# FFN stages of a two-layer encoder: residual sums, load times, the place of the statistics and the order of the last pair

## The chip, the cores and the metric

The kernel runs on one core of a Trainium2 chip in a single launch. The metric is the device time of that launch in microseconds (us). Three runs of the kernel before gave 2211.5, 2214.02 and 2214.56 us, so the median is 2214.02.

## The reference

Two encoder layers run on 512 tokens of width 1024 in float32. Each layer is an FFN at half weight, a mixer (attention of two kinds), cross-attention to a memory of 256 tokens, and a second half-weight FFN, all with an RMS norm ahead and a residual behind:

```python
def rmsnorm(x, g):
    y = xf * lax.rsqrt(jnp.mean(xf * xf, axis=-1, keepdims=True) + EPS)
    return (y * g)
def swiglu(x, wg, wu, wd):
    return (jax.nn.silu(x @ wg) * (x @ wu)) @ wd

for layer in range(2):
    h = h + 0.5 * swiglu(rmsnorm(h, g), wg, wu, wd)          # FFN 1, inner width 2816
    h = h + mixer(rmsnorm(h, mix_g), ...)
    h = h + memory_xattn(rmsnorm(h, mg), rmsnorm(mem, sg), ...)
    h = h + 0.5 * swiglu(rmsnorm(h, g2), wg2, wu2, wd2)      # FFN 2
```

## The kernel before

Activations lie transposed, as eight tiles `x[k]` of 128 features by 512 tokens. Each float32 operand is split into a rounded part and a remainder (`xh` and `xl`, `wh` and `wl`), and a product is three matmuls: high by high, high by low, low by high. ACT makes the high part (for weights L153 or L398, for activations L201), DVE the low part (L155, L399, L203), and in some places POOL takes a share of L155. The two lists `LEAD` and `REST` of the change name these products: (0, 0) and (0, 1) use the weight's high part, (1, 0) its low part.

There are four FFN stages: from 0 to 389 us, from 783 to 1148, from 1148 to 1500 and from 1842 to the end. The mixer and the cross-attention stand between them. A stage has three kinds of work on the tensor engine (PE):

- `plain_pair` computes the first 256 inner features by ordinary matmuls (L309, 128x512): block `b=0` has 48, and `b=1` has 24 for the gate weights `wg` and 24 for `wu`. Between the two halves of `b=1` it calls `stats`: four matmuls by `ident` sum the residual's squares `acc` over the features (`column_sums`, L247), DVE reduces them (L249) and scales them (L256, `v`), and POOL raises `v` to the power -1/2 (L240, `r`). After `b=1`, four more transposes (L318) spread `r` to the tile `R` (L320), by which gate values are multiplied.
- Pairs 1 to 10 use seven products of half-size blocks in place of eight. `open_pair`, `sum_pair`, `cross_pair` and `close_pair` issue one to three products of 24 matmuls (128x256, L417). Their activations are sums and differences of halves of the tokens, made by `token_sums` (L357 `tq`, L361, L364, L366: `t1h`, `t1l` to `t4l`). Their weights are quarters `wq`, loaded by `raw_quarter` (L407) or, for `s1` and `s3`, loaded by SP (L446, L471) and added to by an accumulating DMA of POOL (L447, L473). For `s3`, ACT flips the sign between the two (L472).
- `down` multiplies the finished hidden values `hh` and `hl` by the down weights in three chunks of 8, 8 and 6 inner blocks (L535), eight output blocks `d` in each; L542 and L543 add the result to the residual, and in the last chunk `made` starts the next stage's `xh` and the squares.

The squares are taken by ACT (L216, L219) and added by DVE or POOL (L220) into `acc`. In `out_proj`, at the end of the mixer and of the cross-attention, `sums` does all eight at the end on DVE.

PE follows the program. For DVE, ACT, POOL and SP a scheduler chooses the order, by the order of the program, by priorities (`high_priority`) and by `behind(x)`, which lets an instruction come only after `x`. On each engine the instructions then start in that order. Buffers come round: `wf` has three, `wh` and `wl` two, and `sh` and `sl`, used by every third operand of a pair, one.

Of the kernel before, what the change touches and what calls it, by code (L numbers as in the profile page):

```python
# [19 lines left out]
P = 128  # L20
# [43 lines left out]
PAD_SMALL = 80  # L64

# [37 lines left out]
class Encoder:  # L103
# [45 lines left out]
    def wfill(self, tiles, src, sl, eng, after=None):  # L149
        nc = self.nc  # L150
        w, wh, wl = tiles
        dma = nc.sync.dma_start(w[:, sl], src[:, sl])
# [26 lines left out]
    def load_x(self, srcs):  # L179
# [15 lines left out]
        self.sums()  # L195
# [10 lines left out]
    def sums(self):  # L206

        for x in self.x:
            with self.behind(self.lead), self.behind(self.rest):
                self.acc = self.square(self.acc, x, S, eng=self.nc.vector)  # L210

    def square(self, acc, x, n, pool=None, eng=None):
        nc = self.nc
        if acc is None:
            acc = (pool or self.xp).tile([P, S], F32, name="acc", tag="acc", bufs=1)
            nc.scalar.activation(acc[:, :n], x, AF.Square)  # L216
        else:
            sq = self.xp.tile([P, S], F32, name="sq", tag="sq", bufs=2)
            nc.scalar.activation(sq[:, :n], x, AF.Square)  # L219
            (eng or nc.gpsimd).tensor_add(acc[:, :n], acc[:, :n], sq[:, :n])  # L220
# [18 lines left out]
    def rsqrt(self, out, v, n):  # L239
        self.nc.gpsimd.tensor_tensor(out, v, self.mhalf[:, :n], op=OP.pow)  # L240
# [20 lines left out]
    def ffn(self, pre):  # L261


        with ExitStack() as ctx:
            pool = lambda name: ctx.enter_context(self.tc.tile_pool(name=pre + name, bufs=1))
            f = self.f = SimpleNamespace(pre=pre, hp=pool("h"), tp=pool("t"), H={}, n=0, last=None)
            self.plain_pair()
            if self.mem_r is None:
                self.mem_stats()
            ends = [sum(CHUNKS[:c + 1]) // 2 for c in range(len(CHUNKS))]  # L270
            c = 0
            pair = self.open_pair(1)
            for p in range(1, FB // 2):
                final = p == FB // 2 - 1
                self.sum_pair(pair)
                if p - 1 in [e - 1 for e in ends]:
                    self.down(c)
                    c += 1
                self.cross_pair(pair, final)
                old, pair = pair, None if final else self.open_pair(p + 1)  # L280
                self.close_pair(old, final)
            self.down(c)

    def plain_pair(self):
# [4 lines left out]
        for b in range(2):  # L289
# [3 lines left out]
            pp = [self.bank("pa"), self.bank("pa")] if b == 0 else [self.bank2(), self.bank2()]  # L293
# [11 lines left out]
            for ks, ops in groups:  # L305
                for w, p in zip(ws, pp):
# [133 lines left out]
    def sum_pair(self, pair):  # L440
# [3 lines left out]
        with self.tc.high_priority():  # L444
            pair.s = f.tp.tile([P, 1024], F32, name="s1", tag="s1", bufs=2)
            nc.sync.dma_start(pair.s, self.quarter(p, 3))  # L446
# [9 lines left out]
    def cross_pair(self, pair, final):  # L456
        nc, f, p = self.nc, self.f, pair.p

        def own():
            with self.tc.high_priority():  # L460
                pair.w12 = self.raw_quarter(p, 1)
                w = self.operand(pair.w12)
            x = self.bank("pa")
            self.product(x, w, f.B["21"], True)
            c = self.corner(pair, 0, 0)
            nc.vector.tensor_add(c, c, self.halves(x))

        def other():
            with self.tc.high_priority():
                s = f.tp.tile([P, 1024], F32, name="s3", tag="s3", bufs=2)  # L470
                nc.sync.dma_start(s, self.quarter(p, 2))  # L471
                nc.scalar.activation(s, s, AF.Copy, scale=-1.0)  # L472
                nc.gpsimd.dma_start(s, self.quarter(p, 0), accum_op=OP.add)  # L473
                w = self.operand(s)
            self.product(pair.y, w, f.B["3"], False)
            c = self.corner(pair, 1, 1)
            nc.scalar.copy(c, self.halves(pair.y))
# [1014 lines left out]
```

## Time and profile before

| | |
|---|---|
| median of the runs | 2214.02 us (2211.5 to 2214.56) |
| the profiled execution | 2214.37 us, span 2212.6 us |
| busy: PE, DVE, ACT, POOL | 95%, 71%, 52%, 15% |
| granted clock of the span, mean | 0.984 |

PE is busy in nearly all of the span. The other 5% is idle time of PE, and the profile's list of waits says who ended it. A granted clock of 0.5 is the lower of two levels (1.2 against 2.4 GHz). PE busy time counts modelled ends, so a matmul of 128x512 in a row of its own shows 0.39 us, though the next starts 0.227 us later (24 of them take 5.44 us).

### The profile page before, as it was taken

Reading aid. Unit: us, or ns where it says so; the run is one execution under the profiler, and the core shown is the slowest. Engines: PE = TensorE matmul, PEld = TensorE weight load, DVE = VectorE, ACT = ScalarE, POOL = GpSimd, SP = SyncE. Lnnn points to the kernel's source line nnn. Section 1 sums busy time; section 2 is a strip of 40 time slices with the busy share of each in tenths; the row PEclk is TensorE's granted clock in tenths of the full one; section 3 lists DMA queues with packets and bytes.
Section 4 is the critical chain, followed back from the end, with each engine's and each line's share of the span. In section 5 each row is a group of like instructions: output and inputs, shape, how many; then the busy total and the mean of one; then the engine's idle time right before and its main releaser. Section 6 shows DMA issues by size and latency. Waiting matters only on the chain.

```text
span 2212.6 us, 32535 instructions
## 1 busy us (share of the span) xinstructions
PE 2111.8 (95%) x12830; PEld 1881.5 (85%) x12834; DVE 1573.5 (71%) x2255; ACT 1139.7 (52%) x1701; POOL 339.6 (15%) x306
## 2 busy tenths in 40 slices
PE   4999999999999879999999999999999987999998
PEld 3989998887778769898989899988888876989897
DVE  5767767479876678586788677674668676857666
ACT  4535434465685556253455345344678554635442
POOL 1100001336441100000020000003453011000000
PEclk8999999999999999999999999999999998999999
DMA  6546633421232247375346456334223214546632
GB/s 203 147 128 164 172 105 115 143 81 62 77 122 73 73 124 189 102 186 150 93 137 183 133 162 171 106 110 155 79 86 128 93 58 133 164 123 174 160 103 88
DMA packets 86121, 279.65 MB, mean 126 GB/s; under 512 B 9680, under 2 KB 12880, under 8 KB 85968
## 3 DMA queue, kind: packets, MB, share of 16 engines
q1 hardware_dynamic: 74448, 235.62, 32.1%
q0 software_dynamic: 11520, 41.95, 10.7%
q8 instruction: 101, 1.65, 0.3%
q14 instruction: 52, 0.43, 0.1%
HBM read 271.24 MB, written 6.29 MB: 125 GB/s over the span
## 4 chain that ended last, share of the span: by engine, by line
PE 88%; DVE 7%; DMA 2%; ACT 1%; issue 1%; SPq 0%; DVEq 0%; ACTq 0%
PE ps_pa L417 26%; PE ps_pb L535 11%; PE ps_pa L535 10%; PE ps_pb L417 10%; PE ps_pa L628 10%; PE ps_pa L580 4%; PE ps_pa L309 2%; PE ps_pb L734 2%; PE ps_pa L1166 2%; PE ps_pa L1025 2%; PE ps_pb L786 1%; PE ps_pb L759 1%; PE ps_pa L944 1%; PE ps_pb L309 1%; PE ps_pb L580 1%
## 5 line engine op out<-in xcount | busy, mean ns | idle before, releaser
L153 ACT ACTIVATE wh<-wf 128x1024 fp32r<-128x1024 f32 (+2 forms) x215 | 219.1, 1019 | 380.5 <-PE ps_pb L535 112.7
L155 DVE TENSOR_TENSOR wl<-wf,wh 128x1024 fp32r<-128x1024 f32 (+2 forms) x174 | 202.9, 1168 | 63.6 <-ACT wh L153 62.9
L399 DVE TENSOR_TENSOR wl<-s,wh 128x1024 fp32r<-128x1024 f32 x104 | 127.2, 1223 | 86.5 <-ACT wh L398 64.1
L398 ACT ACTIVATE wh<-s 128x1024 fp32r<-128x1024 f32 x104 | 110.0, 1058 | 114.5 <-PE ps_pb L417 29.4
L398 ACT ACTIVATE wh<-wf 128x1024 fp32r<-128x1024 f32 x84 | 89.1, 1061 | 109.6 <-PE ps_pb L535 23.5
L535 PE MATMUL ps_pb<-hh,wl 128*128 128x512 f32 x352 | 137.8, 392 | 5.4 <-DVE wl L155 5.4
L535 PE MATMUL ps_pa<-hh,wl 128*128 128x512 f32 x352 | 137.8, 392 | 5.4 <-DVE wl L155 5.4
L535 PE MATMUL ps_pb<-hh,wh 128*128 128x512 f32 x352 | 137.6, 391 | 0.0
L535 PE MATMUL ps_pa<-hh,wh 128*128 128x512 f32 x352 | 137.5, 391 | 0.0
L535 PE MATMUL ps_pa<-hl,wh 128*128 128x512 f32 x352 | 137.3, 390 | 0.0
L535 PE MATMUL ps_pb<-hl,wh 128*128 128x512 f32 x352 | 137.3, 390 | 0.0
L155 POOL TENSOR_TENSOR wl<-wf,wh 128x1024 fp32r<-128x1024 f32 x41 | 99.7, 2431 | 176.4 <-ACT wh L153 148.9
L628 PE MATMUL ps_pa<-wh,xh 128*128 128x512 f32 x384 | 123.3, 402 | 0.0
L473 POOL DMA_DIRECT2D s<-l_ffn_wq x40 | 35.6, 890 | 569.2 <-ACT s L472 569.2
L628 PE MATMUL ps_pa<-wh,xl 128*128 128x512 f32 x384 | 119.9, 394 | 0.0
L628 PE MATMUL ps_pa<-wl,xh 128*128 128x512 f32 x384 | 119.5, 393 | 0.0
L542 DVE TENSOR_TENSOR dn<-ps_pb,R 128x512 f32<-128x512 f32 x48 | 33.1, 690 | 100.3 <-PE ps_pb L535 100.3
L542 DVE TENSOR_TENSOR dn<-ps_pa,R 128x512 f32<-128x512 f32 x48 | 33.1, 690 | 100.3 <-PE ps_pa L535 100.3
L447 POOL DMA_DIRECT2D s<-l_ffn_wq x40 | 34.7, 868 | 443.8 <-DMA s<-l_ffn_wq 303.8
L399 DVE TENSOR_TENSOR wl<-wf,wh 128x1024 fp32r<-128x1024 f32 x84 | 102.6, 1222 | 0.0
L399 DVE TENSOR_TENSOR sl<-s,sh 128x1024 fp32r<-128x1024 f32 x56 | 68.5, 1223 | 33.1 <-ACT sh L398 33.0
L628 PEld LDWEIGHTS ps_pa<-wh,xl 128*128 128x128 f32 x384 | 72.7, 189 | 16.0
(372 smaller groups left out, 5946.0 us busy)
## 6 DMA issues: line engine op xcount, KB each, us to landing
wf<-l_ffn_wq SPq DMA_DIRECT2D x120, 512.0 KB, 3.4
s<-l_ffn_wq SPq DMA_DIRECT2D x80, 512.0 KB, 4.2
s<-l_ffn_wq POOLq DMA_DIRECT2D x80, 512.0 KB, 6.8
wf<-l_ffn_wd SPq DMA_DIRECT2D x64, 512.0 KB, 3.8
wf<-l_w_in SPq DMA_DIRECT2D x48, 512.0 KB, 3.2
wf<-l_ffn_wd SPq DMA_DIRECT2D x32, 384.0 KB, 3.1
wf<-l_mem_wkv SPq DMA_DIRECT2D x16, 512.0 KB, 3.2
wf<-l_w_out SPq DMA_DIRECT2D x16, 512.0 KB, 3.3
```

What stands on the lines that cost most here:

```text
L153: nc.scalar.activation(wh[:, sl], w[:, sl], AF.Copy)
L155: eng.tensor_sub(wl[:, sl], w[:, sl], wh.bitcast(F32)[:, sl])
L309: nc.tensor.matmul(p, w[a][:, k * P:(k + 1) * P], xs[k][c], start=k == order[0] and a == c == 0, stop=k == order[-1] and a == 1)
L398: nc.scalar.activation(h, t, AF.Copy)
L399: nc.vector.tensor_sub(l, t, h.bitcast(F32))
L417: self.nc.tensor.matmul(bank[:, sl], w[a][:, o:o + P], xs[k][b], start=first and z == a == b == k == 0, stop=z == a == 1 and k == KB // 2 - 1,
L535: nc.tensor.matmul(bank, w[a][:, j * P:(j + 1) * P], hs[e], start=j == a == e == 0, stop=j == nb - 1 and e == 1)
L542: nc.vector.tensor_mul(t, bank, f.R)
L580: nc.tensor.matmul(banks[dd], a[:, o:o + P], parts(k)[b], start=k == first and a is wh and b == 0, stop=k == last and a is wl)
L628: nc.tensor.matmul(banks[i], xs[k][a][:, i * P:(i + 1) * P], w[b][:, kk * 512:kk * 512 + 512], start=k == a == b == 0, stop=k == KB - 1 an ...
L734: nc.tensor.matmul(bank[:, o:o + n], a, b[:, :n], start=c == 0, stop=c == len(ops) - 1)
L1025: nc.tensor.matmul(banks[c][i], a[:, i * P:(i + 1) * P], b[:, c * 512:(c + 1) * 512], start=(k == 0 and n == 0), stop=(k == KB - 1 and n = ...
```

## The change

- `sums` is called in `out_proj` for four residual tiles at a time, behind their `made`: first for group 1, with the additions on POOL, then for group 0 on DVE. The squares have high priority.
- `token_sums` is called after both blocks of the plain pair, behind the last square and the last addition.
- `stats` comes after the plain pair and no longer between the halves of `b=1`. The part that makes `R` (`plain_end`) is called after `open_pair(1)`.
- The quarter loads (`fetch`) come behind the last load of the plain pair. The memory's statistics (`mem_stats`) come after pair 2.
- The last pair computes "21" (`own`) before "3" as the other pairs do. The first down block of the last chunk goes to `sh` and `sl`, and its eight `LEAD` matmuls come ahead of `close_pair`; the last pair's own operands there all use `wh` and `wl`.
- Inside a chunk the products are grouped: `LEAD` of all inner blocks, then `REST`, then the same for the chunk's last two inner blocks.

```diff
-    def sums(self):
-        for x in self.x:
-            with self.behind(self.lead), self.behind(self.rest):
-                self.acc = self.square(self.acc, x, S, eng=self.nc.vector)
+    def sums(self, xs, eng):
+        with self.behind(self.lead), self.behind(self.rest), self.tc.high_priority():
+            for x in xs:
+                self.acc = self.square(self.acc, x, S, eng=eng)
@@ ffn
-            self.plain_pair()
-            if self.mem_r is None:
-                self.mem_stats()
+            R = self.plain_pair()
...
             pair = self.open_pair(1)
+            R()
...
-                self.cross_pair(pair, final)
-                old, pair = pair, None if final else self.open_pair(p + 1)
-                self.close_pair(old, final)
-            self.down(c)
+                self.cross_pair(pair)
+                if final:
+                    early = self.block(c, 0, True)
+                    self.down_products(c, early, LEAD, False)
+                    self.close_pair(pair, True)
+                    self.down(c, early)
+                else:
+                    old, pair = pair, self.open_pair(p + 1)
+                    self.close_pair(old, False)
+                if p == 2 and self.mem_r is None:
+                    self.mem_stats()
@@ plain_pair
-                    if b == 1 and p is pp[0]:
-                        v, r = self.stats(self.acc, QB)
-            if b == 0:
-                with self.behind(self.lead), self.behind(self.rest):
-                    self.token_sums()
-        p = self.bank2()
+        f.after = self.loaded
+        with self.behind(self.summed), self.behind(self.squared):
+            self.token_sums()
+        v, r = self.stats(self.acc, QB)
+        return lambda: self.plain_end(banks, r)
@@ quarter loads
+    def fetch(self, t, p, q):
+        with self.behind(self.f.after):
+            self.nc.sync.dma_start(t, self.quarter(p, q))
+        return t
@@ down
-        early = [block(d) for d in range(2)]
-        for w, bank in early:
-            products(bank, w, range(nb - 2))
-        for d, (w, bank) in enumerate(early):
-            products(bank, w, range(nb - 2, nb))
-            done(d, bank)
+        early = [first or self.block(c, 0), self.block(c, 1)]
+        for b in early[first is not None:]:
+            self.down_products(c, b, LEAD, False)
+        for b in early:
+            self.down_products(c, b, REST, False)
+        for d, b in enumerate(early):
+            self.down_products(c, b, LEAD + REST, True)
+            done(d, b[1])
@@ out_proj
+            if done:
+                self.sums(self.x[4 * g:4 * g + 4], nc.gpsimd if g else nc.vector)
...
-        self.sums()
```

SP issues the loads of the first stage in this order before (`wf` from `l_ffn_wq` and every `s_` tile are quarters of the pairs):

```order
L193 DMA x<-xT 128x512
L471 DMA s_545<-l_ffn_wq 128x1024
L193 DMA x<-xT 128x512
L471 DMA s_777<-l_ffn_wq 128x1024
L152 DMA wf<-l_ffn_wg 128x512
L193 DMA x<-xT 128x512
L125 DMA cols<-cols 128x92
L193 DMA x<-xT 128x512
L446 DMA s_452<-l_ffn_wq 128x1024
L152 DMA wf<-l_ffn_wu 128x512
L446 DMA s_684<-l_ffn_wq 128x1024
L152 DMA wf<-l_ffn_wg 128x1024
```

The same place, the first loads of SP, now:

```order
L195 DMA x<-xT 128x512
L127 DMA cols<-cols 128x92
L195 DMA x<-xT 128x512
L154 DMA wf<-l_ffn_wg 128x512
L195 DMA x<-xT 128x512 x2
L154 DMA wf<-l_ffn_wu 128x512
L195 DMA x<-xT 128x512
L154 DMA wf<-l_ffn_wg 128x1024
L195 DMA x<-xT 128x512 x2
L154 DMA wf<-l_ffn_wg 128x512
L154 DMA wf<-l_ffn_wu 128x512
L195 DMA x<-xT 128x512
```

The four `s_` loads have left the head of SP's queue; they now stand behind the last load of `wu`, which is two rows further on.

In the second FFN stage (l0_ffn2), DVE had this order between the token sums and `R` before:

```order
L364 TENSOR_TENSOR t3l<-tq,t3h 128x1024
L357 SCALAR_TENSOR_TENSOR tq<-x,cols,tq 128x256 x3
L399 TENSOR_TENSOR wl<-wf,wh 128x1024
L220 TENSOR_TENSOR acc<-acc,sq 128x512
L364 TENSOR_TENSOR t2l<-tq,t2h 128x1024
L364 TENSOR_TENSOR t4l<-tq,t4h 128x1024
L220 TENSOR_TENSOR acc<-acc,sq 128x512 x3
L249 TENSOR_REDUCE s<-ps_pb 128x4
L256 TENSOR_SCALAR v<-s 128x4
L399 TENSOR_TENSOR wl<-s_7711,wh 128x1024
L320 COPY R<-ps_pb 128x512
```

DVE at the same place now, where the additions into `acc` have all gone before:

```order
L375 TENSOR_TENSOR t3l<-tq,t3h 128x1024
L411 TENSOR_TENSOR wl<-wf,wh 128x1024
L375 TENSOR_TENSOR t2l<-tq,t2h 128x1024
L411 TENSOR_TENSOR wl<-s_7711,wh 128x1024
L251 TENSOR_REDUCE s<-ps_pb 128x4
L375 TENSOR_TENSOR t4l<-tq,t4h 128x1024
L466 TENSOR_TENSOR s_7711<-s_7711,wf 128x1024
L411 TENSOR_TENSOR wl<-wf,wh 128x1024
L258 TENSOR_SCALAR v<-s 128x4
L411 TENSOR_TENSOR sl<-s_7711,sh 128x1024
L503 TENSOR_TENSOR s_7711<-wf,s_7711 128x1024
L331 COPY R<-ps_pb 128x512
```

The additions have gone from the place ahead of the reduce, and weight remainders, one of them of the accumulated tile `s_7711`, have come ahead of the reduce and of `v`.

At the end of the first stage (l0_ffn1), ACT had this order in the last pair before (128x768 are down weights, `gu` are products copied out of PSUM, the second L344 and L507 belong to the pair's second half):

```order
L153 ACTIVATE wh<-wf 128x768
L507 ACTIVATE t<-gs 128x512
L153 ACTIVATE wh<-wf 128x768
L490 COPY gu<-ps_pa 128x2x256
L344 ACTIVATE hh<-gs 128x512
L507 ACTIVATE t<-gs 128x512
L344 ACTIVATE hh<-gs 128x512
L153 ACTIVATE wh<-wf 128x768 x2
```

ACT at the same place now:

```order
L488 COPY gu<-ps_pa 128x2x256
L155 ACTIVATE wh<-wf 128x768 x2
L516 ACTIVATE t<-gs 128x512
L499 COPY gu<-ps_pa 128x2x256
L355 ACTIVATE hh<-gs 128x512
L516 ACTIVATE t<-gs 128x512
L355 ACTIVATE hh<-gs 128x512
L155 ACTIVATE wh<-wf 128x768
```

The weights of a second and a third down block are both converted ahead of the first `t` of the last pair, where one stood ahead of it before.

## Rows read from the trace of the kernel before

**Rows 1.** The page: busy time, share of the span, instructions of each engine.

```profile
PE 2111.8 (95%) x12830; PEld 1881.5 (85%) x12834; DVE 1573.5 (71%) x2255; ACT 1139.7 (52%) x1701; POOL 339.6 (15%) x306
```

**Rows 2.** Waits of PE, whole span: us in total, times, longest.

```profile
PE ps_pb L247 <- DVE acc L220: 38.8, 5, 10.3
...
PE ps_pa L535 <- DVE wl L155: 5.4, 6, 1.0
PE ps_pb L535 <- DVE wl L155: 5.4, 6, 1.0
PE ps_pa L417 <- ACT gu L454: 4.8, 4, 1.2
```

**Rows 3.** Stretch 0 to 31: us, engines' busy time, clock, DMA share, GB/s.

```profile
0.00:31.00 31.00, 11.61 (x28) 7.86 (x29) 8.68 (x21) 11.65 (x17) 4.30 (x10) 0.87 0.93 277
```

**Rows 4.** Timeline of SP, first stage: start, us, operation.

```profile
17.41 0.33 SPq L193 DMA_DIRECT2D x<-xT  x1
...
30.03 0.33 SPq L152 DMA_DIRECT2D wf<-l_ffn_wu  x1
```

**Rows 5.** Timeline of PE, first stage; in brackets idle time and its releaser.

```profile
51.34 1.09 PE L247 MATMUL ps_pb<-ident,acc 128*128 128x128 f32 x4 [9.19 <-DVE acc L220]
...
65.06 0.64 PE L417 MATMUL ps_pb<-t1h,wh 128*128 128x256 f32 x4
```

**Rows 6.** Timeline of DVE, third stage (l1_ffn1).

```profile
1152.60 6.03 DVE L357 SCALAR_TENSOR_TENSOR tq<-x,cols,tq 128x256 f32<-128x256 f32 x15
...
1163.48 1.22 DVE L364 TENSOR_TENSOR t2l<-tq,t2h 128x1024 fp32r<-128x1024 f32 x1
...
1166.88 0.68 DVE L249 TENSOR_REDUCE s<-ps_pb 128x4 f32<-128x512 f32 x1
```

**Rows 7.** Timeline of POOL, third stage.

```profile
1154.30 0.88 POOL L447 DMA_DIRECT2D s<-l_ffn_wq  x1 [5.15 <-DVE tq L357]
...
1167.86 1.03 POOL L240 TENSOR_TENSOR r<-v,mhalf 128x4 f32<-128x4 f32 x1 [5.90 <-DVE v L256]
```

**Rows 8.** Timeline of PE, second, third and fourth stage.

```profile
812.86 1.11 PE L247 MATMUL ps_pb<-ident,acc 128*128 128x128 f32 x4 [10.34 <-DVE acc L220]
...
824.57 0.64 PE L417 MATMUL ps_pb<-t1h,wh 128*128 128x256 f32 x4
...
1176.07 0.64 PE L417 MATMUL ps_pb<-t1h,wh 128*128 128x256 f32 x4
...
1883.74 0.64 PE L417 MATMUL ps_pb<-t1h,wh 128*128 128x256 f32 x4
```

**Rows 9.** Stretch with the lower clock behind the stall of the second stage.

```profile
807.80:818.00 10.20, 5.14 (x14) 4.22 (x15) 5.31 (x8) 1.26 (x2) 1.04 (x1) 0.50 0.01 2
```

**Rows 10.** Timeline of PE, cross-attention of both layers.

```profile
728.50 1.11 PE L247 MATMUL ps_pb<-ident,acc 128*128 128x128 f32 x4 [4.90 <-DVE acc L220]
...
1787.59 1.11 PE L247 MATMUL ps_pb<-ident,acc 128*128 128x128 f32 x4 [4.63 <-DVE acc L220]
```

**Rows 11.** Timeline of PE, chunks and last pair of the first stage.

```profile
143.65 0.50 PE L535 MATMUL ps_pb<-hh,wl 128*128 128x512 f32 x1 [0.94 <-DVE wl L155]
...
355.27 0.40 PE L535 MATMUL ps_pb<-hh,wh 128*128 128x512 f32 x1
...
364.79 0.50 PE L535 MATMUL ps_pb<-hh,wl 128*128 128x512 f32 x1 [0.74 <-DVE wl L155]
```

**Rows 12.** Timeline of ACT, last pair of the first stage.

```profile
354.04 0.63 ACT L507 ACTIVATE t<-gs 128x512 f32<-128x512 f32 x1 [4.16 <-DVE gs L505]
355.04 0.85 ACT L153 ACTIVATE wh<-wf 128x768 fp32r<-128x768 f32 x1 [0.37 <-PE ps_pa L417]
...
358.38 0.63 ACT L507 ACTIVATE t<-gs 128x512 f32<-128x512 f32 x1 [1.49 <-DVE gs L505]
...
360.50 0.63 ACT L344 ACTIVATE hh<-gs 128x512 fp32r<-128x512 f32 x1 [1.49 <-DVE gs L509]
```

**Rows 13.** Issues of DMAs, 1149 to 1163: size, median us to landing.

```profile
s<-l_ffn_wq POOLq DMA_DIRECT2D x4, 512.0 KB, 11.5
```

More of the change, by code (lines that the diff above doesn't have):

```diff
@@ L64 @@
 PAD_SMALL = 80
+LEAD, REST = ((0, 0), (0, 1)), ((1, 0),)
 CHUNKS = (8, 8, 6)
@@ L454, in sum_pair, with cross_pair @@
         nc.scalar.copy(self.corner(pair, 0, 1), self.halves(pair.y))
-    def cross_pair(self, pair, final):
+    def cross_pair(self, pair):
         nc, f, p = self.nc, self.f, pair.p
[L459 to L477, printed above, removed]
-            nc.vector.tensor_add(c, c, self.halves(pair.z))
-        for step in (other, own) if final else (own, other):
-            step()
+        with self.tc.high_priority():
+            pair.w12 = self.raw_quarter(p, 1)
+            w = self.operand(pair.w12)
+        x = self.bank("pa")
+        self.product(x, w, f.B["21"], True)
+        c = self.corner(pair, 0, 0)
+        nc.vector.tensor_add(c, c, self.halves(x))
+        with self.tc.high_priority():
+            s = f.tp.tile([P, 1024], F32, name="s3", tag="s3", bufs=2)
+            self.fetch(s, p, 2)
+            nc.scalar.activation(s, s, AF.Copy, scale=-1.0)
+            nc.gpsimd.dma_start(s, self.quarter(p, 0), accum_op=OP.add)
+            w = self.operand(s)
+        self.product(pair.y, w, f.B["3"], False)
+        c = self.corner(pair, 1, 1)
+        nc.scalar.copy(c, self.halves(pair.y))
+        nc.vector.tensor_add(c, c, self.halves(pair.z))
     def close_pair(self, pair, final):
         nc, f, p = self.nc, self.f, pair.p
+        own = False if final else None
         def lower():
             with self.tc.high_priority():
-                w = self.operand(self.raw_quarter(p, 3))
+                w = self.operand(self.raw_quarter(p, 3), own)
             self.product(pair.y, w, f.B["4"], False)
@@ L494, in upper @@
                 nc.vector.tensor_sub(pair.s, pair.w12, pair.s)
-                w = self.operand(pair.s)
+                w = self.operand(pair.s, own)
             self.product(pair.z, w, f.B["22"], False)
@@ L521, in close_pair, with block, down_products, down @@
         self.hidden_parts(p, gs, 0)
[L523 removed]
+    def block(self, c, d, own=False):
         nc, f = self.nc, self.f
[L527 to L538 removed]
+        n = CHUNKS[c] * P
+        src = self.I[f.pre + "wd"][d, :, sum(CHUNKS[:c]) * P:sum(CHUNKS[:c]) * P + n]
+        if not own:
+            return self.wload(src, n), self.bank2()
+        with self.tc.high_priority():
+            w = self.wp.tile([P, 1024], F32, name="wf", tag="wf", bufs=3)
+            h, l = [f.tp.tile([P, 1024], F32R, name=t, tag=t, bufs=1) for t in ("sh", "sl")]
+            self.wfill((w, h, l), src, slice(0, n), nc.vector)
+        return (h, l), self.bank2()
+    def down_products(self, c, block, ops, tail):
+        f = self.f
+        (w, bank), nb = block, CHUNKS[c]
+        for a, e in ops:
+            for j in range(nb - 2, nb) if tail else range(nb - 2):
+                b = sum(CHUNKS[:c]) + j
+                h = f.H[b // 2][e][:, b % 2 * S:b % 2 * S + S]
+                self.nc.tensor.matmul(bank, w[a][:, j * P:(j + 1) * P], h, start=j == a == e == 0,
+                                      stop=j == nb - 1 and (a, e) == ops[-1])
+    def down(self, c, first=None):
+        nc, f = self.nc, self.f
+        last = c == len(CHUNKS) - 1
         def done(d, bank):
```

57 lines of the change are left out of this document (26 added, 31 removed).

## The prediction

> **What bounds the kernel now.** I read the page first: PE is busy for 2111.8 of 2212.6 us [rows 1], so a change that adds no matmul is worth at most the idle time of PE and the time that its lower clock costs. The list of waits then says who ended that idle time [rows 2]. The largest item, 38.8 us in five waits, are the four transposes of L247, which wait for the last addition into `acc`. Next come 10.8 us in twelve waits for the low part `wl` of a down weight, and 4.8 us in four for a copy of the product "2" in the last pair. A matmul count is unchanged by the edit, so I take the stages one at a time, each by the moment when PE starts the product T1 (`ps_pb<-t1h`), the first that needs all of the stage's statistics to be out of its way.
>
> **Start of the first stage.** DMA is busy for 0.93 of the first 31 us at 277 GB/s [rows 3]; 4.2 MB of that are the four `s` loads and their four accumulating loads. The last `x` is issued at 17.41 and the last `wu` at 30.03 [rows 4]. Then the squares are added late among the token sums, PE stands 9.19 us, and T1 starts at 65.06 [rows 5]. Now `x`, `cols`, `wg` and the first `wu`, 3.6 MB in all, go first. At 277 GB/s and some 2 us for the first to land they need 3.6 / 0.277 + 2 = 15 us. The last `xh` and `xl` are then ready at about 17, block `b=0` ends near 22.5 and `b=1` (10.9 us) near 34, with its column sums behind it at 34.6 and `open_pair` (24 matmuls, 2.88 us) at 37.3. No stall for `acc` is left. What is late next is `R`: between the last addition (near 26) and `v`, DVE now has 16 `tq` at 0.40, nine instructions of 1024 columns at 1.14 from one start to the next, and the reduce at 0.68 [rows 6], that is 6.4 + 10.3 + 0.7 = 17.4, so 43.5 at the earliest. ACT must feed them in its own order, behind two `s3` loads and three memory tiles, for which I add 2 us. With 1.03 for the power on POOL [rows 7], T1 starts near 46.5, after a new PE stall of some 9 us. That is 18.5 us sooner. A stall of that length was followed by 0.50 of the clock for 10.2 us, half of it in the stall [rows 9], so 2.5 us are lost again: **-16 us**, and between -10 (ACT held by the loads) and -27 (`R` hidden behind `open_pair`, T1 at 38).
>
> **Start of both second FFN stages.** T1 starts at 824.57 and 1883.74, after stalls of 10.34 us [rows 8] and 9.7 (38.8 less the other four of its five waits) for `acc`. The additions now follow the last `xl` (near 790) on DVE, four at 0.69 with two weights of 1.2 between, and are done near 795.7, so `b=1` follows `b=0` without a gap: it ends near 805.6, `open_pair` near 809.5. DVE's queue again holds `v` back: from 795.7, 16 `tq` (6.4), nine of 1024 columns (10.3), and the reduce (0.7) make 813.1, one of the nine waits for ACT's conversion behind `open_pair` (+1), and the power takes 1.03, so T1 starts near 817. The stall changes its place and shrinks from 10.3 to some 7. 7.5 us sooner, less 2.5 of clock, is **-5** for the first; the second's stall was 0.6 shorter, and I take **-4**. Each lies between 0 and -14. The third stage, l1_ffn1, had no stall for `acc`. There the reduce comes to stand behind a weight that needs the end of `b=1`, so T1 stays at 1176.07 [rows 8] within a microsecond: 0.
>
> The accumulating DMA is the cover that can fail here. In the third stage, where the `s` loads already follow the last `wu`, POOL issues the first accumulation at 1154.30, 4 us after the `s` load, and it lands 11.5 us later by the median [rows 7, 13]. In l0_ffn2 the `s` loads would go out near 790.6, when `b=0` frees a buffer for the last `wu`, so `s1` is whole near 806, and DVE reaches its `wl` near 808: 2 us to spare.
>
> **Cross-attention.** PE waits 4.90 and 4.63 us for `acc` [rows 10], and for the half clock behind them I add 1.6 and 1.4, part of the 2.5 that followed the longer stall. With four additions on POOL ahead and four on DVE early, `acc` is whole when PE comes, by my count to within a microsecond. **-6.5 and -6**; if POOL is late with its weights, half of that.
>
> **Chunks.** In chunks 1 and 2 PE waits 0.94 [rows 11] and 1.0 at the second matmul of the third block, since `wl` is used there. With LEAD first, `wl` is used 12 matmuls (2.7 us) later, so the wait goes. Over four stages 4 x 1.94 = **-7.8**. Nothing else is late there, as `wh` was ready.
>
> **The last pair.** Two waits go: 1.2 for the copy, since "21" now stands between, and 0.76 at the last chunk [rows 11], as the second block no longer shares a buffer with the first. But the cover of the last gate half is shorter. Before, 24 matmuls (5.4 us) ran from 355.27 until `hh` was needed, and `hh` was done at 361.13 [rows 11, 12], just in time. Now eight have moved ahead, and 16 (3.63 us) are left. Furthermore ACT's order puts two weight conversions before the first `t`, and the second needs the buffer that the product "4" frees at its end, E. The row of before at 355.04 shows that such a conversion waits for PE at the head of ACT's queue [rows 12]. From E: the conversion 0.85, on DVE its `wl` 0.95, which stands ahead of `t` there, two steps of 0.69, `hh` 0.63, then `hl` and `gs` 1.4, `t` 0.63, two steps 1.4, and the second `hh` 0.63, with 0.3 for the semaphores: E + 8.1. PE needs it at E + 3.63 + 0.23. The stall is 4.2, and 0.2 more for `hl`: 4.4 in place of 1.96, that is +2.4 in each stage, **+9.8**. If the clock falls behind it, as it did after 4.63, up to 2 more each (+8). The other end is the chain of before, 5.9 us from E, a stall of 2.0: 0.
>
> The Trainium skill states in "Perfetto Trace Analysis" (Tensor Engine Instruction) that ACT, DVE and GpSimd are strict FIFO. It speaks against this change at this place: by it the `t` waits for the end of product "4" though its own input is there. If ACT could pass the waiting conversion, the last pairs would come to 0 and the whole to about 2169. The row at 355.04 agrees with the rule as far as it goes; what stands behind the conversion there needed the same event.
>
> **The memory's statistics** (eight squares, seven additions) leave the start for pair 2, with ACT 52% and POOL 15% busy [rows 1]: 0. POOL's and DVE's shares of `wl` in the mixers shift by one tile in places, 1.2 us either way at single blocks: 0, within 4.
>
> **Sum.** -16 - 5 - 4 - 12.5 - 7.8 + 9.8 = -35.5. The profiled execution took 2214.4, which is 0.4 over the median: **2179 us**.
>
> **Rivals.**
> - *R is no longer waited for.* If DVE and ACT run through the start without waits, T1 comes at the end of `open_pair`: -27, -14, -13 in the three stages, and no half clock. With the rest as above 2214.4 - 54 - 12.5 - 7.8 + 9.8 = 2150. For it: the third stage, with its statistics in the middle, starts T1 without a stall for `acc`, so DVE can keep up where nothing is added to its queue. Against it: seven instructions stand ahead of `v` that did not before. Half of it gives 2164.
> - *The stalls only change place.* The starts gain 10, 0 and 0, one cross-attention keeps half of its wait (3), and the half clock follows each last pair (+8): 2214.4 - 10 - 9.5 - 7.8 + 17.8 = 2205. For it: 2 us to spare at `s1`, and a stall of over 4 us in each last pair.
> - *Slower: the accumulated quarter holds DVE.* `wl<-s1` stands ahead of the reduce, in order. From the point where `s1` lands more than 2 us after my count, each microsecond moves `R`, and PE with it, in the three starts. To lose 35.5 us and more it has to be 12 + 2 us later in each, 29 us from the load's issue in place of 15; the time would be 2220. Against it: the 11.5 us of [rows 13] were under a full load of the third stage.
> - *It doesn't do what it says.* If loads still crowd the start and POOL's additions come as late as DVE's did, the last pairs' +9.8 cancels the chunks' -7.8 and the time stays at 2214.
>
> **Chances.** The forecast, 2168 to 2192, 0.52; R not waited for, 2150 to 2168, 0.19; stalls change place, 2192 to 2209, 0.22; slower 0.04; no effect 0.03. A measurement of this kernel tells 0.2% (4.4 us) from no change. So faster 0.93, same 0.03, slower 0.04. The range 2160 to 2202 leaves out the outer part of both neighbours.
>
> **What would show it.** In the profile after: T1 near 46.5, 817 less what was gained before, and the same for the fourth stage; PE idle before L329's transposes, released by POOL's `r`, and none before L249; no wait for `wl` in the chunks but one of some 4 us for `hh` at the end of each stage, with ACT's second `wh` starting when product "4" ends. The first step fails if the last `x` lands after 20 us or PE waits for DMA at T1; the forecast is wrong if the four last pairs stall under 2 or over 7 us, or if the new stall at `R` exceeds 12.

## The result and the profile after

The changed kernel takes 2184.72 us (median of 4 runs, 2184.33 to 2187.51) against 2213.43 for the kernel before on the same chip: 0.9874 of it, with an interval from 0.9857 to 0.9891, or 28.7 us less. The profiled execution took 2184.71 us with a span of 2182.9. The page of after gives PE less busy time than in [rows 1] and a larger share of the span:

```profile
PE 2105.0 (96%) x12834; PEld 1881.6 (86%) x12834; DVE 1571.6 (72%) x2242; ACT 1138.4 (52%) x1701; POOL 361.1 (17%) x319
```

The waits of PE (us in total, times, longest) show what took the place of [rows 2]:

```profile
PE ps_pb L329 <- POOL r L242: 25.6, 4, 12.5
PE ps_pa L553 <- ACT hh L355: 14.9, 4, 3.7
...
PE ps_pb L432 <- DVE gu L489: 3.0, 4, 0.7
PE ps_pb L249 <- DVE acc L222: 2.9, 2, 2.5
```

The 38.8 us for `acc` have become 2.9. The 10.8 us for `wl` and the 4.8 for the product "2" are gone. New are 25.6 us for `r`, 14.9 for the last pair's `hh`, and 3.0 for `gu` at the last pair's product "22".

To see where the time went I set the same products of both traces side by side (T1, T2 and so on of every pair) and read by how much the later trace leads. Each piece of the program then has one number:

| piece | forecast | measured |
|---|---|---|
| start of the first stage, up to T2 | -16 | -13.2 (T1 alone -15.5) |
| eight chunks with two blocks ahead (1 and 2 of each stage) | -7.8 | -10.8 |
| four last pairs with the third chunk | +9.8 | +16.9 (3.6, 5.0, 3.7, 4.6) |
| cross-attention, layers 0 and 1 | -6.5, -6 | -6.5, -4.0 |
| starts of l0_ffn2 and l1_ffn2 | -5, -4 | -6.5, -5.8 |
| l1_ffn1's start and both mixers | 0 | 0.0 |
| sum | -35.5 | -29.9 |

The spans differ by 29.7. The 0.0 is a sum of small pieces: the mixer of layer 0 lost 0.5, the memory's column sums in pair 2 another 0.2, and l1_ffn1's start and the mixer of layer 1 gained 0.3 each.

**First stage.** The timeline of PE (start, us, operation; in brackets the idle time ahead and its releaser) answers to [rows 5]:

```profile
32.82 0.60 PE L249 MATMUL ps_pb<-ident,acc 128*128 128x128 f32 x4
...
48.80 1.11 PE L329 MATMUL ps_pb<-ident,r 128*128 128x128 f32 x4 [12.52 <-POOL r L242]
49.57 1.20 PE L432 MATMUL ps_pb<-t1h,wh 128*128 128x256 f32 x4
```

The plain pair ends at 32.8, where the forecast had 34, and no time is lost at `acc`. All that is left stands at `r`. ACT and DVE show why it comes at 48.8 and not at 45:

```profile
29.54 0.42 ACT L218 ACTIVATE acc<-mem 128x256 f32<-128x256 f32 x1 [3.27 <-DMA mem<-memT]
...
35.73 1.04 ACT L372 ACTIVATE t1h<-tq 128x1024 fp32r<-128x1024 f32 x1
```

```profile
36.81 1.22 DVE L377 SCALAR_TENSOR_TENSOR t1l<-tq,t1h 128x1024 fp32r<-128x1024 f32 x1 [3.85 <-ACT t1h L372]
...
46.55 0.16 DVE L258 TENSOR_SCALAR v<-s 128x4 f32<-128x4 f32 x1
```

Three squares of the memory stand ahead of `t1h` on ACT, each waits for its load (3.27, 1.57 and 2.51 us, 7.35 together), and DVE in turn stands 3.85 us for `t1h`. Behind `t1l` ten more instructions of DVE come before `v`. The power on POOL behind `v` took 1.95 us, where [rows 7] have 1.03.

**Second FFN stage.** PE, and DVE between the reduce and `v` (with [rows 8]):

```profile
797.58 1.11 PE L329 MATMUL ps_pb<-ident,r 128*128 128x128 f32 x4 [6.06 <-POOL r L242]
```

```profile
791.31 0.70 DVE L251 TENSOR_REDUCE s<-ps_pb 128x4 f32<-128x512 f32 x1
791.91 1.23 DVE L375 TENSOR_TENSOR t4l<-tq,t4h 128x1024 fp32r<-128x1024 f32 x1
793.04 1.24 DVE L466 TENSOR_TENSOR s<-s,wf 128x1024 f32<-128x1024 f32 x1
794.18 1.24 DVE L411 TENSOR_TENSOR wl<-wf,wh 128x1024 fp32r<-128x1024 f32 x1
795.31 0.18 DVE L258 TENSOR_SCALAR v<-s 128x4 f32<-128x4 f32 x1
```

Three instructions of 1.13 us each, from one start to the next, hold `v` back for 3.4 of the 6.06 us. They were in the order printed ahead of the prediction. Another 0.9 is the power, which takes 1.95 us here too, beside an instruction of DVE that had begun 0.18 us before it:

```profile
795.40 1.23 DVE L411 TENSOR_TENSOR sl<-s,sh 128x1024 fp32r<-128x1024 f32 x1
795.58 1.95 POOL L242 TENSOR_TENSOR r<-v,mhalf 128x4 f32<-128x4 f32 x1 [10.86 <-DVE v L258]
```

The same holds at the starts of the first and the fourth stage (both 1.95). Before, the power took 1.04 at all three, and DVE stood idle. Why it takes longer is not shown.

The two starts of FFN 2 also gained at a place that the forecast did not look at. Before, PE waited 2.04 us for `xh` at the first products of l0_ffn2 (2.01 at l1_ffn2). On ACT two sign flips of `s3` stood among the eight `xh`:

```profile
782.86 1.06 ACT L472 ACTIVATE s<-s 128x1024 f32<-128x1024 f32 x1
```

```profile
785.53 0.50 PE L309 MATMUL ps_pa<-xh,wh 128*128 128x512 f32 x1 [2.04 <-ACT xh L201]
```

With the quarter loads behind the last `wu`, the flips come later, and the longest wait there is 0.44 (0.45 at l1_ffn2). At matched products this is 1.8 of the 6.5 us in l0_ffn2 and some 2 of the 5.8 in l1_ffn2.

**Cross-attention of layer 1.** The wait of [rows 10] has shrunk from 4.63 to 2.51 us there, and to 0.37 in layer 0:

```profile
1763.68 0.66 PE L249 MATMUL ps_pb<-ident,acc 128*128 128x128 f32 x4 [2.51 <-DVE acc L222]
```

DVE, ahead of it, has the last additions between the next step's low parts:

```profile
1760.61 0.68 DVE L222 TENSOR_TENSOR acc<-acc,sq 128x512 f32<-128x512 f32 x1
1761.21 0.68 DVE L1116 TENSOR_TENSOR xql<-ps_pa,xqh 128x512 fp32r<-128x512 f32 x1
1761.82 1.21 DVE L157 TENSOR_TENSOR wl<-wf,wh 128x1024 fp32r<-128x1024 f32 x1
1762.95 0.68 DVE L222 TENSOR_TENSOR acc<-acc,sq 128x512 f32<-128x512 f32 x1
```

**Chunks.** In the first chunk, where [rows 11] had 0.94 us for `wl`, the third block now runs through:

```profile
142.85 1.52 PE L553 MATMUL ps_pa<-hh,wl 128*128 128x512 f32 x6
```

**Last pair of the first stage**, PE, ACT and DVE (for ACT before, [rows 12]):

```profile
334.88 0.74 PE L432 MATMUL ps_pb<-xh,wh 128*128 128x256 f32 x4 [0.74 <-DVE gu L489]
...
344.39 0.45 PE L553 MATMUL ps_pa<-hh,sh 128*128 128x512 f32 x1
348.57 0.80 PE L553 MATMUL ps_pa<-hh,sh 128*128 128x512 f32 x1 [3.73 <-ACT hh L355]
```

```profile
340.46 0.85 ACT L155 ACTIVATE wh<-wf 128x768 fp32r<-128x768 f32 x1 [2.03 <-PE ps_pa L432]
341.21 0.62 ACT L516 ACTIVATE t<-gs 128x512 f32<-128x512 f32 x1
...
347.89 0.63 ACT L355 ACTIVATE hh<-gs 128x512 fp32r<-128x512 f32 x1 [1.49 <-DVE gs L518]
```

```profile
339.53 0.68 DVE L514 TENSOR_TENSOR gs<-gu,R 128x512 f32<-128x512 f32 x1
```

DVE has the first `t`'s input ready at 340.21, but ACT stands at a conversion (2.03 us in all) whose buffer the product "4" frees at E = 340.46, and the `t` starts only behind it, at 341.21. The second `hh` ends at 348.52, which is E + 8.06; the forecast had E + 8.1.

Stretches at the lower clock (us, busy time by engine, clock, DMA share, GB/s) behind the stall at `r` of the first stage and behind the last pairs of the first and second, with [rows 9]:

```profile
41.00:54.70 13.70, 5.90 (x28) 5.90 (x29) 11.19 (x13) 5.64 (x10) 7.29 (x8) 0.50 0.26 87
348.20:351.60 3.40, 3.03 (x7) 2.41 (x8) 1.18 (x2) 0.32 (x1) 0.00 (x0) 0.51 0.00 0
1095.80:1102.60 6.80, 6.02 (x14) 4.72 (x15) 3.06 (x6) 2.36 (x4) 0.00 (x0) 0.50 0.00 0
```

In each of them PE stands for a part of the time and then works on at 0.50, 1.2 in place of 2.4 GHz. The one behind the stall at `r` of the second stage lasted 6.8 us as well.

### The profile page after: what moved, and what is told of

Read it like the earlier page. It is cut to its first block, busy times and chain, and to the rows that moved or that the text cites. A ratio compares the mean times of both kernels' runs of the same rounds, so it can differ in the third digit from the quotient of the medians.

```text
span 2182.9 us, 32518 instructions
## 1 busy us (share of the span) xinstructions
PE 2105.0 (96%) x12834; PEld 1881.6 (86%) x12834; DVE 1571.6 (72%) x2242; ACT 1138.4 (52%) x1701; POOL 361.1 (17%) x319
## 3 DMA queue, kind: packets, MB, share of 16 engines
q0 software_dynamic: 11520, 41.95, 10.8%
## 5 line engine op out<-in xcount | busy, mean ns | idle before, releaser
L411 DVE TENSOR_TENSOR wl<-s,wh 128x1024 fp32r<-128x1024 f32 x108 | 132.1, 1223 | 70.6 <-ACT wh L410 70.6
L462 POOL DMA_DIRECT2D s<-l_ffn_wq x40 | 35.5, 887 | 448.5 <-DMA s<-l_ffn_wq 356.8
L553 PE MATMUL ps_pb<-hh,wh 128*128 128x512 f32 x352 | 97.2, 394 | 0.0
L553 PE MATMUL ps_pb<-hl,wh 128*128 128x512 f32 x352 | 96.7, 393 | 0.0
L553 PE MATMUL ps_pb<-hh,wl 128*128 128x512 f32 x352 | 96.4, 392 | 0.0
L222 POOL TENSOR_TENSOR acc<-acc,sq 128x512 f32<-128x512 f32 (+1 forms) x37 | 46.6, 1260 | 268.1 <-ACT sq L221 267.1
L553 PE MATMUL ps_pa<-hh,wh 128*128 128x512 f32 x328 | 89.7, 392 | 0.0
L553 PE MATMUL ps_pa<-hh,wl 128*128 128x512 f32 x328 | 88.7, 389 | 0.0
L553 PE MATMUL ps_pa<-hl,wh 128*128 128x512 f32 x328 | 88.7, 389 | 0.0
```

The lines of the kernel that those rows point to most:

```text
L222: self.summed = (eng or nc.gpsimd).tensor_add(acc[:, :n], acc[:, :n], sq[:, :n])
L411: nc.vector.tensor_sub(l, t, h.bitcast(F32))
L462: nc.gpsimd.dma_start(pair.s, self.quarter(p, 2), accum_op=OP.add)
L553: self.nc.tensor.matmul(bank, w[a][:, j * P:(j + 1) * P], h, start=j == a == e == 0, stop=j == nb - 1 and (a, e) == ops[-1])
```

## The experiments

All kernels are the changed one with the edit shown, except e4, which is the kernel before with one part of the change; "..." marks code left out. Ratios are to the kernel before; the changed kernel stands at 0.9874.

**e1: the conversion leaves the head of ACT's queue.** The third down block's `wh` comes behind the last pair's second `hh`.

```diff
+    f.made = nc.scalar.activation(hh[:, sl], h, AF.Copy)
...
-    nc.scalar.activation(wh[:, sl], w[:, sl], AF.Copy)
+    with self.behind(act): nc.scalar.activation(wh[:, sl], w[:, sl], AF.Copy)
...
-    b = self.block(c, d)
+    b = self.block(c, d, act=f.made if last and d == 2 else None)
```

> The changed kernel with one thing moved: ACT converts the weights of the last chunk's third down block behind the last pair's second hh, and no longer ahead of the first tanh. Theory A (strict order on ACT: the tanh waits behind a conversion that waits for product 4): the tanh starts near 340.3 in place of 341.2, the second hh ends some 1.4 us sooner (347.1 in place of 348.5), the stall of 3.7 us shrinks to 2.0 to 2.5 in each of the four stages, and the half clock behind it goes; the time is 2174 to 2179. Theory B (only the shorter cover of 16 matmuls counts, the tanh's inputs are late anyway): the stall stays at 3.7 and the time at 2185.

Measured: 2175.24 us (2173.77 to 2175.9), 0.9829 [0.9815, 0.9844]. ACT and PE in its first stage:

```profile
338.75 0.63 ACT L516 ACTIVATE t<-gs 128x512 f32<-128x512 f32 x1 [1.83 <-DVE gs L514]
```

```profile
345.78 0.51 PE L553 MATMUL ps_pa<-hh,sh 128*128 128x512 f32 x1 [2.50 <-ACT hh L355]
```

The `t` now starts when its own input is there, and the stall falls from 3.73 to 2.50 in all four stages. That the chain hung on the waiting conversion is shown. It is also what the Trainium skill says in "Perfetto Trace Analysis" (Tensor Engine Instruction), that ACT is a strict FIFO; the trace of the changed kernel agrees, as the `t` stood for 1.0 us (340.21 to 341.21) with its input ready. The shorter waits are 4.9 of the 9.5 us. The lower clock behind the four last pairs lasted 10.2 us in all, where the changed kernel has 20.4, so it did not go altogether as expected. What remains of the stall, 2.5 us, is the chain itself, which has too few matmuls beside it.

**e2: the eight leading matmuls back behind the last pair.**

```diff
-    self.down_products(c, early, LEAD, False)
     self.close_pair(pair, True)
+    self.down_products(c, early, LEAD, False)
```

> The changed kernel with the eight LEAD matmuls of the first down block issued behind close_pair, so that 24 matmuls in place of 16 lie between product 4 and the last pair's hh. Theory A (the stall at hh is chain minus cover): the stall at hh falls from 3.7 to about 1.9, but the wait of product 22 for the addition L489 grows from 0.74 to about 2.6, so the idle sum stays at 4.5 in each stage; what is gained is only the half clock (idle in two pieces), 4 to 8 us in all: 2177 to 2181. Theory B (the eight matmuls cover nothing ahead of product 22): the 0.74 stays and the time falls by 4 x 1.8 and the clock, to 2170 to 2174.

Measured: 2184.51 us (2176.84 to 2185.6), 0.9865 [0.9845, 0.9885], the same as the changed kernel. PE in the first stage, and the clock behind the first wait:

```profile
334.73 1.23 PE L432 MATMUL ps_pb<-xh,wh 128*128 128x256 f32 x4 [2.58 <-DVE gu L489]
...
349.74 0.50 PE L553 MATMUL ps_pa<-hh,sh 128*128 128x512 f32 x1 [1.98 <-ACT hh L355]
```

```profile
334.30:337.70 3.40, 2.97 (x14) 2.97 (x15) 0.37 (x1) 0.00 (x0) 0.00 (x0) 0.50 0.42 120
```

The eight matmuls only choose which wait they cover: 0.74 + 3.73 became 2.58 + 1.98. Expected was a gain from the clock, and in the sum it did not come. The lower clock fell behind the shorter waits too, in the first and the fourth stage. Behind the four last pairs it lasted 10.2 us in place of 20.4, but in the rest of the profiled run 10.2 us longer than in the changed kernel, behind waits that both have.

**e3: the quarter loads early again.**

```diff
-        f.after = self.loaded
+        f.after = None
```

> The changed kernel with the quarter loads not held behind the last wu load. Theory A (the first stage gained because its x and weights no longer share the DMA engines with 4 MB of quarters): the last x lands near 28 again, T1 of the first stage starts 10 to 14 us later than 49.6, the two second FFN stages stay within 1.5 us; time 2195 to 2200. Theory B (the gain came from taking the squares and the statistics out of the way): T1 of the first stage stays within 3 us; time 2183 to 2188.

Measured: 2200.84 us (2198.06 to 2201.52), 0.9944 [0.9927, 0.996], so the later loads are worth 16 of the 28.7 us. SP and PE in its first stage:

```profile
29.50 0.33 SPq L154 DMA_DIRECT2D wf<-l_ffn_wu  x1
```

```profile
28.68 1.65 PE L317 MATMUL ps_pa<-xh,wh 128*128 128x512 f32 x3 [7.09 <-ACT wh L155]
...
61.47 1.20 PE L432 MATMUL ps_pb<-t1h,wh 128*128 128x256 f32 x4
```

The last `wu` is issued at 29.50 again [rows 4], PE stands 7.09 us for an operand in the middle of the plain pair, and T1 starts 11.9 us later than in the changed kernel. The second stage lost 2.2 us at its start, more than the 1.5 expected. There the wait for `xh` is back:

```profile
780.71 0.75 PE L317 MATMUL ps_pa<-xh,wh 128*128 128x512 f32 x1 [2.01 <-ACT xh L203]
```

So the later loads are also what took that wait away.

**e4: the grouping of the chunks alone, on the kernel before.**

```diff
-                for a, e in ((0, 0), (1, 0), (0, 1)):
-                    nc.tensor.matmul(bank, w[a][:, j * P:(j + 1) * P], hs[e], ...)
+            for a, e in ops:
+                for j in js: ...
...
-            products(bank, w, range(nb - 2))
+            products(bank, w, range(nb - 2), LEAD)
+        for w, bank in early:
+            products(bank, w, range(nb - 2), REST)
```

> The kernel before with one part of the change alone: LEAD of all inner blocks, then REST, in all chunks (the last pair otherwise as before). Theory A (a stall costs the whole shift from one matmul's start to the next, 1.35 us, where the trace shows 0.94 to 1.0 of idle time): minus 4 x 2 x 1.35 in chunks 1 and 2 and minus 4 x 1.0 in chunk 3, so 2198 to 2200. Theory B (a stall costs its idle time): minus 7.8 and minus 3.0, so 2202 to 2204.

Measured: 2201.21 us (2197.97 to 2202.49), 0.9945 [0.9931, 0.996], 12 us. The time lies between the two expectations; the matched products decide. Each of the eight chunks gives 1.35 us at the next of them, 10.8 in all, and the third chunks give some 0.6 each. The forecast took the idle time of [rows 11], 0.94, which counts from a modelled end. From start to start the same place of before, 142.21 to 143.65 with 0.23 due, loses 1.2.

**e5: the third down block's first twelve matmuls ahead of all that needs the last `hh`.** Its conversion comes behind the copy of product "4".

```diff
-            nc.scalar.copy(self.corner(pair, 1, 0), self.halves(pair.y))
+            f.copied = nc.scalar.copy(self.corner(pair, 1, 0), self.halves(pair.y))
...
+        third = self.block(c, 2, act=f.copied) if last else None
...
+        if third: self.down_products(c, third, LEAD + REST, False); early.append(third)
```

> The changed kernel with the third down block's twelve first matmuls (2.7 us) issued ahead of the last pair's hh, its weights converted by ACT behind the copy of product 4 and so behind the first tanh. Theory A (stall at hh = chain after product 4 minus the matmuls that cover it): chain 6.5 to 7.5 us, cover 28 x 0.227 + 0.23 = 6.6, so the stall falls from 3.7 to under 1 in each stage and no half clock follows; the time falls by 4 x (3 + 1 to 2) to 2164 to 2170. Theory B (each step put ahead delays the chain as much, as ACT and DVE are the bound there): the stall stays over 2.5 and the time over 2174.

Measured: 2161.47 us (2158.92 to 2162.82), 0.9765 [0.975, 0.9779]. ACT in the first stage:

```profile
340.89 0.63 ACT L355 ACTIVATE hh<-gs 128x512 fp32r<-128x512 f32 x1 [1.49 <-DVE gs L518]
```

The second `hh` ends at 341.5, and PE, with twelve more matmuls to do, has no wait for it in any of the four stages; the lower clock there is gone too. The profiled runs differ by 25.8 us; 5.9 of them stand at T2 of the first stage, where the memory's third tile landed at 28.7 in place of 35.3 (`t1h` at 29.14, the stall at `r` 7.42). Nothing was changed there, so this part cannot be put down to the edit. Whether it belongs to the run or to the kernel, one profile of each does not tell. The other 19.9 are in the main the last pairs and the clock behind them.

**e6: the memory's squares behind the first tanh.**

```diff
-                with self.behind(powed):
+                with self.behind(powed), self.behind(self.plain_t):
```

> The changed kernel with ACT's squares of the memory behind the first tanh of the first stage. Theory A (in the first stage the chain to R is held by ACT, which waits at the memory's tiles for their loads, 3.9 us of DVE idle before t1l): R and T1 come 3.5 to 4 us sooner (T1 near 45.7 in place of 49.6), other stages unchanged; time 2179 to 2182. Theory B (DVE's instructions ahead of v set it): under 1 us; 2184 to 2186.

Measured: 2181.72 us (2180.3 to 2183.38), 0.9858 [0.9843, 0.9872]. The first part on ACT:

```profile
27.74 1.06 ACT L372 ACTIVATE t1h<-tq 128x1024 fp32r<-128x1024 f32 x1 [1.11 <-DVE tq L368]
```

It starts 8 us sooner, the stall at `r` falls from 12.52 to 9.77, and T2 starts 4.4 sooner, of which 3.7 are left two products on. So the memory's tiles held that start back, but for less than a third of the stall: the next loads, of quarters, are late as well (ACT waits 3.03 and 3.90 us for two of them).

**e7: reduce and `v` ahead of the low parts of T2 and T4 and of the weights of T1 and T2.** `f.scaled` is the instruction that makes `v`.

```diff
+        v, r = self.stats(self.acc, QB); f.scaled = self.scaled
         with self.behind(self.summed), self.behind(self.squared):
             self.token_sums()
-        v, r = self.stats(self.acc, QB)
...
-        T2 = parts("t2", t2)
+        with self.behind(f.scaled): T2 = parts("t2", t2)
...
-        T4 = parts("t4", t4)
+        with self.behind(f.scaled): T4 = parts("t4", t4)
...
-            w = self.operand(pair.s)
+            with self.behind(f.scaled if p == 1 else None): w = self.operand(pair.s)
```

> The changed kernel with the reduce and v of the residual's statistics ahead of t2l, t4l and the weights of T1 and T2 on DVE. Theory A (the new stall at R is DVE's order alone): in both second FFN stages PE's stall of 6.0 us at R falls under 1.5 and T1 comes 4.5 to 6 us sooner with less half clock; in the first stage 2 to 4 us; in the third up to 1; time 2166 to 2172. Theory B (what is put behind v is then late for T1 and T2 itself): the stall at R goes but PE waits as long for the operands; time over 2180.

Measured: 2188.92 us (2187.65 to 2192.02), 0.9895 [0.9878, 0.9911], so nothing is won. PE in the second FFN stage:

```profile
791.28 0.65 PE L329 MATMUL ps_pb<-ident,r 128*128 128x128 f32 x4 [0.29 <-POOL r L242]
...
796.57 0.74 PE L432 MATMUL ps_pa<-t2h,sh 128*128 128x256 f32 x4 [1.75 <-ACT sh L410]
...
800.57 1.22 PE L432 MATMUL ps_pa<-t2h,sl 128*128 128x256 f32 x4 [2.45 <-DVE sl L411]
```

`r` is in time, and PE stands at T2's weights instead. This order only moves the wait.

**e8: all of `out_proj`'s additions on DVE.**

```diff
-    self.sums(self.x[4 * g:4 * g + 4], nc.gpsimd if g else nc.vector)
+    self.sums(self.x[4 * g:4 * g + 4], nc.vector)
```

> The changed kernel with all additions of the squares in out_proj on DVE (four of eight, three of them on POOL, before). Theory A (the share on POOL is what takes the wait for acc away): acc is whole some 2 us later in both cross-attentions, the waits grow from 0.4 and 2.5 to 2 to 2.5 and 4 to 4.6, in the two second FFN stages 0 to 1 us; time 2188 to 2191. Theory B (moving the squares ahead is enough, and POOL's additions slow DVE's xl from 0.75 to 1.5 us): no change or faster; 2181 to 2185.

Measured: 2186.02 us (2185.25 to 2187.96), 0.9878 [0.9863, 0.9893], not to be told from the changed kernel. The waits for `acc` are 0.22 in place of 0.37 in layer 0 and 3.70 in place of 2.51 in layer 1. What moved the waits from 4.9 and 4.6 is then the early call with high priority (which of these two was not tried); POOL's share adds about 1 us in one place.

**e9: only what PE needs last behind `v`.** The statistics come ahead of the token sums as in e7, but behind `v` stand only T4's sums and low part and the subtraction for T2's weight.

```diff
+        v, r = self.stats(self.acc, QB); f.scaled = self.scaled
         with self.behind(self.summed), self.behind(self.squared):
             self.token_sums()
-        v, r = self.stats(self.acc, QB)
...
-            nc.vector.tensor_sub(pair.s, pair.s, pair.w11)
+            with self.behind(f.scaled if p == 1 else None): nc.vector.tensor_sub(pair.s, pair.s, pair.w11)
...
-        T4 = parts("t4", t4)
+        with self.behind(f.scaled): T4 = parts("t4", t4)
```

> As e7_stats_first, but only what T2 and T4 need (the subtraction for T2's weights, the sums and the low part of T4) is put behind v; t2l and T1's weights stay ahead of the reduce. Theory A (e7 lost because t2l and T1's weights were pushed back as well): the stall at R of the second FFN stages falls from 6.0 to under 1, PE then waits 1 to 2.5 us for T2's weights, T2 starts 3.5 to 6 us sooner in each of the two and in the first stage 3 to 5; time 2170 to 2177. Theory B (DVE has no room there: whatever passes behind v comes back as a wait at T2): T2 starts within 2 us of where it does now; time 2182 to 2188.

Measured: 2174.6 us (2168.89 to 2176.89), 0.9823 [0.9808, 0.9838], 10 us better than the changed kernel. PE in the second FFN stage:

```profile
791.63 0.65 PE L329 MATMUL ps_pb<-ident,r 128*128 128x128 f32 x4 [2.42 <-POOL r L242]
```

The stall at `r` is 2.42 there and 2.31 in the fourth stage, without a new one at T2, so those 3.4 us of DVE's queue were a matter of order and not a lack of time. At matched products these two starts give 4.2 and 3.6 us and the first stage 6.1. Of the latter, 2.2 are loads that came sooner (`t1h` at 33.5 in place of 35.7), which the edit does not touch; from `t1l` to `v` DVE took 6.3 us in place of 9.7. Between the first and the second stage 3.8 went back, with no new wait: the lower clock lasted longer behind waits that both kernels have. Two such stretches of e9, behind 3.73 us for `hh` and 1.54 in the cross-attention:

```profile
341.60:348.40 6.80, 5.91 (x14) 4.61 (x15) 3.06 (x6) 2.54 (x4) 0.00 (x0) 0.50 0.10 39
730.80:734.20 3.40, 3.40 (x11) 2.72 (x10) 1.62 (x5) 2.79 (x9) 0.08 (x1) 0.50 0.00 0
```

In the changed kernel the first lasts 3.4 us and the second is missing.

**e10: e5 and e6 together.** 

> e5_third_block and e6_mem_late together. If the two places are independent the gains add: 2161.5 - 3.5 = 2157 to 2159. If the memory's squares, now later on ACT, meet the chunks or pairs, the time is over 2161.

Measured: 2161.79 us (2159.3 to 2162.02), 0.9769 [0.9753, 0.9785], the same as e5 alone. The two do not add. In both profiled runs ACT waits next for the accumulated quarter, 2.52 us in e5 and 4.24 in e10, and converts it at 33.66 and 33.91. In e5 the tiles that e6 takes out of the way had landed early as well.

**e11: e5, e6 and e9 together.** 

> e5_third_block, e6_mem_late and e9_v_at_once together. Theory A of e9: 2144 to 2152, T2 of the first stage near 47 in place of 54.8. Theory B of e9: 2157 to 2163.

Measured: 2147.98 us (2147.12 to 2151.77), 0.971 [0.9695, 0.9724]; it beats both kernels. The largest of its waits of PE:

```profile
PE ps_pb L329 <- POOL r L242: 13.1, 4, 7.6
```

The wait for `hh` is gone from all four stages, and the one for `r` is half of what it was. From e10 to e11 only e9's edit is added, for 13.8 us by the medians. The profiled spans differ by 11.1, of which the first stage has 0.8. So here that order gained nearly all of it behind the first stage, at the two starts of FFN 2 above all, and the loads of the start have next to no part in it. T2 of the first stage starts at 49.0, not at 47. What holds it then are quarters: ACT, and behind it DVE, wait for the accumulated one, and DVE stands another 1.75 us for the next.

```profile
34.23 1.06 ACT L410 ACTIVATE wh<-s 128x1024 fp32r<-128x1024 f32 x1 [4.38 <-DMA s<-l_ffn_wq]
```

```profile
35.32 1.22 DVE L411 TENSOR_TENSOR wl<-s,wh 128x1024 fp32r<-128x1024 f32 x1 [2.14 <-ACT wh L410]
```

## Why the prediction came out as it did

The forecast was 2179, with 2160 to 2202 as its range; 2184.72 lies inside, 5.7 above, and the likeliest case is the one that came. No step took the wrong direction. But that the sum is so near is partly luck: several terms were mis-sized, and they cancel. The last pairs, the first stage and the cross-attention came out 7.1, 2.8 and 2.0 worse than forecast, the chunks and the two starts 3.0, 1.5 and 1.8 better.

**The last pairs (+9.8, measured +16.9).** This is the largest miss, and it has the sign of the whole error. The mechanism was right to a tenth of a microsecond (E + 8.06) and is shown by e1. The stall itself was even smaller than forecast, 3.95 us from start to start in place of 4.4. But the price was put at 2.4 a stage, against 4.2 measured. From start to start the wait for `hh` costs 348.57 - 344.39 - 0.23 = 3.95, the one at 334.88 costs 0.9, and the seven matmuls after 348.57 run 1.5 us longer than 0.23 each at the lower clock: 6.35 in all, less some 2.4 for the two waits of before, is 4.0. Behind the stalls of the second and fourth stage the lower clock lasted 6.8 us, which is why these two lost 5.0 and 4.6. I had named the clock as an upper end only. And I had not seen the wait for `gu`: product "22" needs DVE's addition behind a `wl`, and the eight matmuls ahead of it do not cover that. Both were inside the upper end (+17.8).

**The chunks (-7.8, measured -10.8).** The cause was right (e4); the idle time was taken as the price, and the price is a third larger.

**The first stage (-16, measured -13.2).** The loads were right: `b=1` ends at 32.8, and e3 gives 10.8 of the 13.2 back at T2. The stall at `r` was not: some 9 us were forecast, and 12.52 came, which is over the 12 that I had set as a sign of being wrong. The 2 us that I added for ACT behind loads were 7.35 on ACT and 3.85 on DVE, and the power took 1.95. T1 started at 49.57 and not near 46.5. The lower clock lasted 13.7 us, not 10.2, and took back 2.3 between T1 and T2, where the forecast had 2.5.

**Starts of the second FFN stages (-5 and -4, measured -6.5 and -5.8).** The stall moved from `acc` to `r` and shrank to 6.06, where I had some 7. (The terms that I added up, 813.1 + 1 + 1.03, make 815.1, not the 817 that I wrote.) The stalls account for 4.7 and 3.7 of the gains, near the forecast; the rest is the wait for `xh`, which the sum left out. e9 shows 3.6 of the 6.06 to be a matter of order. In the changed kernel the accumulated quarter was never waited for, so the rival in which it holds DVE is out there. In the first stage of e11, with the rest out of the way, it does hold DVE.

**Cross-attention (-6.5 and -6, measured -6.5 and -4.0).** Layer 1 keeps 2.51 us. The reservation was POOL being late with weights. What the trace shows is DVE: two instructions, 1.9 us, between the last two additions. The one term for both layers was right in layer 0 alone. Whether these two could wait was not tried.

**l1_ffn1 and the mixers (0, measured 0.0).** As forecast, up to 0.5 in single places; the new wait of 1.01 for `r` in l1_ffn1 cost nothing that can be seen at the next products.

Of the rivals, "R is no longer waited for" failed in all four stages. With `r` in time T2's weights are late in e7, and in the best order tried, e9's, the second and fourth stage still stall for 2.42 and 2.31, so its 27 + 14 + 13 us were not reached in any run. "The stalls only change place" held for the last pairs alone.

## What to carry to other kernels

When matmuls are moved ahead of a chain, count what is left to cover it behind, and look at what stands at the head of the queue of the engine that makes the last operand: a conversion there that waits for a buffer blocks everything after it. Price a PE stall from start to start, and add the time at the lower clock behind it, even when the stall is only 2 to 4 us. Before moving a result forward in a queue, ask what is due next. Putting behind `v` only what T2 and T4 need gained 10 us here (13.8 on top of e10); putting `t2l` and T1's weights behind it as well gained none.

## What was not expected of the hardware

- The granted clock fell to 0.50 behind waits of 2.58 us (e2) and even 1.54 (e9), and for equal waits of 3.73 it stayed low for 3.4 us in two stages of the changed kernel and for 6.8 in the other two. What a short wait costs in clock can be told from no single profile.
- The same power of 128x4 on POOL took 1.95 us at three stage starts of the changed kernel, where an instruction of DVE over 128x1024 had just begun, and 1.01 to 1.04 wherever else `r` of this size was made in that trace and in the one of before.
- Beside POOL's additions of 128x512 in the first cross-attention, DVE's `xl` took twice as long. Two rows of after, of DVE and of POOL:

```profile
699.93 3.11 DVE L205 SCALAR_TENSOR_TENSOR xl<-x,cols,xh 128x512 fp32r<-128x512 f32 x2
```

```profile
698.11 4.38 POOL L222 TENSOR_TENSOR acc<-acc,sq 128x512 f32<-128x512 f32 x3 [3.03 <-ACT sq L221]
```

  They took 1.40 and 1.78 us, where such an `xl` takes 0.74 or 0.75 in most places of the trace. In e8, with these additions on DVE, both took 0.74.
- An unchanged start of the program varied between the profiled runs: the stall at `r` was 12.52, 12.17, 11.80 and 7.42 us in after, e1, e2 and e5, and the memory's third tile landed at 35.3, 35.1, 35.2 and 28.7.
